# Ordering the small RWKV products G and Yo by operand shape, and alternating partition halves in M, TK and gy

## The chip, the core and the metric

One core of a Trainium2 chip runs the whole program. The metric is device time in microseconds (us) from one launch; the kernel before was timed three times, and one more execution was profiled. A core has a matrix engine (TensorE; PE in the rows, with its weight loads shown as PEld), a vector engine (DVE), a scalar engine (ACT), a third elementwise engine (POOL) and a queue engine (SP) that issues most DMAs. Each engine works through its own instruction list in order and waits on semaphores for the others. Products are written to PSUM, from where DVE and ACT read them.

## What is computed

One transformer layer on a sequence of 256 tokens with model width 2048: an input projection, four mixers (GLA, RG-LRU, NSA and RWKV-7), a gated merge, an output projection and a convolutional FFN. Nearly all of the arithmetic is in the big projections. The change lies in two mixers. RWKV-7 has 8 heads of width 64 and a state that is updated token by token:

```python
def step(state, inp):
    r_t, w_t, k_t, v_t, kk_t, a_t = inp
    sa = jnp.einsum('bhij,bhj->bhi', state, -kk_t)
    state = (state * w_t[:, :, None, :] + sa[..., None] * (kk_t * a_t)[:, :, None, :]
             + v_t[..., None] * k_t[:, :, None, :])
    return state, jnp.einsum('bhij,bhj->bhi', state, r_t)
```

GLA computes, chunk by chunk, `scores = einsum('bhtd,bhsd,bhtsd->bhts', qi, ki, decay)`; of it only one level of block scores (the tile gy) is touched.

## The kernel before

The projections stream weight chunks of 512 KB from HBM (`raw`). Each half chunk is split by ACT into a high part (`wh`, line 327) and by DVE into the rest (`wl`, line 328), and PE multiplies both with the activations into the tile `acc` (`group_A`). These acc products come in pairs: one of 512 columns with `wh`, one of 256 with `wl`. They fill PE for most of the program.

The RWKV recurrence is done in four chunks c = 0 to 3 of 64 tokens. The heads lie as 4 groups j times 2 partition halves par (partitions 0 to 63 and 64 to 127, the slices `H`). `rwkv_pre(c)` makes what does not depend on the state: M (per half, four products of 64 rows and 128 columns, masked by DVE into `mt`), and TK (transposes of the decayed keys, copied by ACT into `tk`). `rwkv_chain(c)` is the serial part. G is the sum of a product of `mt` with `uv` (128 rows, 64 columns) and, from c = 1 on, of `ar` (in the rows: ops) with the state `st` (64 rows, 64 columns); ACT copies it; U multiplies it with `z`; DVE and ACT copy U into `uv`; S gives the state's increment, from which DVE makes the new `st`; Yo is the output, again a sum of a product of 128 rows (`mt`) and, from c = 1 on, one of 64 rows (`st`). G and Yo each have 8 products of either kind in a chunk with state, and in chunk 0 only the 8 of 128 rows. `rwkv_pre(c + 1)` is written ahead of `rwkv_chain(c)`.

These small products are float32, and the trace shows each of them twice: 8 products are x16 in a row of the trace, once x8 in the printed instruction lists.

A scheduler sets the order on every engine: instructions carry priorities by band (loads, weight splits, evacuations, mixers, big products), and the scheduler places them by its own estimate of the time. So the mixers' products stand between the acc products, at places that can move when the source changes. Small PSUM tiles come from a pool of four banks (`self.ps`), acc tiles from another.

The lines of the profile that matter: 297 (every product through `mm`), 813 (TK), 289 (DVE tensor-tensor through `tt`, among them the new `st`), 327 and 328 (the splits), 831 (ACT's copy of G), 836 and 837 (the two copies of U into `uv`), 860 (the copy of Yo).

Of the kernel before, what the change touches and what calls it, by code (L numbers as in the profile page):

```python
# [16 lines left out]
MULT, ADD, SUB = ALU.mult, ALU.add, ALU.subtract  # L17
# [208 lines left out]
class Kern:  # L226
# [547 lines left out]
    def rwkv_pre(self, c, T):  # L774
        nc = self.nc
        ar, bk = T["ar"], T["bk"]
        cs = slice(c * 64, c * 64 + 64)
        H = (slice(0, 64), slice(64, 128))
        mt = self.sb("m4", [P, 2, 4, 128], F32, "mt")
        mask = self.cst("mM").unsqueeze(1).broadcast_to([P, 4, 128])  # L780
        for par in range(2):
            h = H[par]
            ps = self.ps("M")
            for j in range(4):
                self.mm(ps[:, j * 128:(j + 1) * 128], bk[h, j, par:par + 2, :].rearrange("p a b -> p (a b)"),
                        ar[h, j, :, :].rearrange("p a b -> p (a b)"))
            self.tt(mt[:, par], ps.rearrange("p (j t) -> p j t", j=4), mask, MULT)
        T["mt"] = mt
        T["z"], T["mt"] = self.rw_z[:, 4 * c:4 * c + 4, :], mt

        uv = self.sb("m2", [P, 4, 2, 64], F32, "uv")
        nc.gpsimd.memset(uv[0:64, :, 0, :], 0.0)
        nc.gpsimd.memset(uv[64:128, :, 1, :], 0.0)
        idn = self.cst("ident")
        for par in range(2):
            for f in range(2):
                for t in range(2):
                    o = 64 * (1 - par) + 32 * t
                    nc.vector.transpose(uv[o:o + 32, :, par, 32 * f:32 * f + 32],
                                        self.rw_v[64 * par + 32 * f:64 * par + 32 * f + 32, :, c * 64 + 32 * t:c * 64 + 32 * t + 32])  # L800
        T["uv"] = uv
        if c < 3:
            ec = self.rw_ec[:, :, c:c + 1]
            ht = self.sb("m4", [P, 4, 3, 64], F32, "ht")
            self.tt(ht[:, :, 0:2, :].rearrange("p j a s -> p j (a s)"), bk[:, :, 0:2, :].rearrange("p j a s -> p j (a s)"),
                    ec.broadcast_to([P, 4, 128]), MULT)
            nc.scalar.copy(ht[64:128, :, 2, :], ht[64:128, :, 0, :])
            tk = self.sb("m2", [P, 2, 4, 64], F32, "tk")
            for par in range(2):
                h = H[par]  # L810
                ps = self.ps("TK")[:, 0:256].rearrange("p (j d) -> p j d", j=4)
                for j in range(4):
                    nc.tensor.transpose(ps[:, j, :], ht[h, j, par:par + 2, :].rearrange("p a b -> p (a b)"), idn[h, h])
                nc.scalar.copy(tk[:, par], ps)
            T["tk"] = tk
        return T

    def rwkv_chain(self, c, T, st):
        nc = self.nc
        H = (slice(0, 64), slice(64, 128))  # L820
        ar, mt, z, uv = T["ar"], T["mt"], T["z"], T["uv"]
        g4 = lambda n: self.ps(n)[:, 0:256].rearrange("p (j s) -> p j s", j=4)
        ps = g4("G")
        for j in range(4):
            for par in range(2):
                h = H[par]
                self.mm(ps[h, j, :], mt[:, par, j, 0:64], uv[:, j, par, :], start=True, stop=(st is None))
                if st is not None:
                    self.mm(ps[h, j, :], ar[h, j, 0, :], st[h, j, :], start=False, stop=True)
        g = self.m1("G")  # L830
        nc.scalar.copy(g, ps)
        ps = g4("U")
        for j in range(4):
            for h in H:
                self.mm(ps[h, j, :], z[h, j, :], g[h, j, :])
        nc.vector.tensor_copy(uv[0:64, :, 0, :], ps[0:64])
        nc.scalar.copy(uv[64:128, :, 1, :], ps[64:128])
        new = None
        if c < 3:
            tk = T["tk"]  # L840
            ps = g4("S")
            for j in range(4):
                for par in range(2):
                    self.mm(ps[H[par], j, :], tk[:, par, j, :], uv[:, j, par, :])
            new = self.sb("st", [P, 4, 64], F32, "st")
            if st is None:
                nc.vector.tensor_copy(new, ps)
            else:
                sd = self.m1("sd")
                ec = self.rw_ec[:, :, c:c + 1]  # L850
                self.tt(sd, st, ec.broadcast_to([P, 4, 64]), MULT)
                self.tt(new, sd, ps, ADD)
        ps = g4("Yo")
        for j in range(4):
            for par in range(2):
                h = H[par]
                self.mm(ps[h, j, :], uv[:, j, par, :], mt[:, par, j, 64:128], start=True, stop=(st is None))
                if st is not None:
                    self.mm(ps[h, j, :], st[h, j, :], ar[h, j, 1, :], start=False, stop=True)
        nc.scalar.copy(self.rw_y[:, :, c * 64:c * 64 + 64], ps)  # L860
        return new

# [174 lines left out]
    def gla(self):  # L1037
        nc = self.nc
        H = (slice(0, 64), slice(64, 128))
        qk, b = self.gl_qk, self.gl_b  # L1040
        t = self.m4("glt")
# [3 lines left out]
        st = [self.m1("gst", 4) for _ in range(2)]  # L1045
        idb = self.cst("eye64").unsqueeze(1).broadcast_to([P, 4, 64])

        def scores(Q, K):
            out = [self.ps("gs")[:, 0:256].rearrange("p (a t) -> p a t", a=4) for _ in range(2)]
            for j in range(2):  # L1050
                for tl in range(2):
                    for odd in range(2):
                        for par in range(2):
                            o = odd ^ par
                            sl = slice(tl * 128 + 64 * o, tl * 128 + 64 * o + 64)
                            self.mm(out[par][H[o], 2 * j + tl, :], K[H[par], j, sl], Q[H[par], j, sl])
            return out

        ps = scores(qk[:, 0:2, :], qk[:, 2:4, :])
        for par in range(2):  # L1060
            self.tt(st[par], ps[par], idb, MULT)
        blk, st = st, [self.m2("gst", 4) for _ in range(2)]
# [3 lines left out]
        for lv in range(8):  # L1066
            m = 1 << lv
            bv = b.rearrange("p j (n m) -> p (j n) m", m=2 * m)
            e = self.m2("ge")
            ev = e.rearrange("p j (n m) -> p (j n) m", m=2 * m)  # L1070
            self.tt(ev, bv, bv[:, :, m - 1:m].broadcast_to([P, 256 // m, 2 * m]), SUB)
            self.act(e, e, AF.Abs)
            self.act(e, e, AF.Exp, scale=-1.0 / 16)
            qe = self.m4("qe")
            self.tt(qe[:, 0:2, :], qk[:, 0:2, :], e, MULT)
            self.tt(qe[:, 2:4, :], qk[:, 2:4, :], e, MULT)
            if lv == 6:
                for par in range(2):
                    h = H[par]
                    ps = self.ps("gy")[0:64, 0:256].rearrange("p (a t) -> p a t", a=4)  # L1080
                    for j in range(2):
                        for tl in range(2):
                            s0 = tl * 128
                            self.mm(ps[:, 2 * j + tl, :], qe[h, 2 + j, s0:s0 + 64], qe[h, j, s0 + 64:s0 + 128])
                    nc.vector.tensor_copy(st[par][0:64, :, 64:128], ps)
            elif lv < 6:
                ps = scores(qe[:, 0:2, :], qe[:, 2:4, :])
                mask = self.gm[:, lv:lv + 1, :].broadcast_to([P, 4, 64])
                for par in range(2):
                    nc.vector.copy_predicated(blk[par], mask, ps[par])  # L1090
                    if lv == 5:
                        for o, h in enumerate(H):
                            nc.scalar.copy(st[par][h, :, 64 * o:64 * o + 64], blk[par][h])
            else:
                for par in range(2):
                    h = H[par]
                    ps = self.ps("gx")[:, 0:256].rearrange("p (j t) -> p j t", j=2)
                    for j in range(2):
                        self.mm(ps[:, j, :], qe[h, 2 + j, 0:128], qe[h, j, 128:256])
                    nc.scalar.copy(sx[:, 2 * par:2 * par + 2, :], ps)  # L1100
        o = self.m4("go")
        v = self.gl_v
        for j in range(2):
            ps = self.ps("go")
# [449 lines left out]
```

## Time and profile before

| | |
|---|---|
| time, three runs | 1580.47, 1581.78, 1582.03 us (median 1581.78) |
| the profiled execution | 1582.63 us, of which 1580.8 us from first to last instruction |
| PE busy | 1562.0 us (99%) |
| DVE, ACT busy | 1238.8 us (78%), 962.7 us (61%) |
| mean granted TensorE clock | 0.991 |

The profile is of one execution. A matmul's row shows its start and how long it was under way; matmuls overlap, so a stretch in which PE is called busy may hold many products or few. What a group of products costs is read from its first start to the start of the next group. PEclk is the granted clock as a share of full speed (1.00 is 2.4 GHz, 0.50 is 1.2 GHz).

### The profile page before, as it was taken

What the parts mean: (1) busy time and instruction counts of PE and PEld (TensorE: products, weight loads), DVE (VectorE), ACT (ScalarE), POOL (GpSimd) and SP (SyncE); (2) the same over time, 40 slices, a digit from 0 to 9 for tenths busy, and PEclk for the clock granted to TensorE, in tenths of its full rate; (3) what the DMA queues carried; (4) which work ended last, traced back from release to release, by engine and by line L of the source; (5) the groups of instructions that cost most, each with busy time, mean ns of one, the idle gap of its engine ahead of it and who ended that gap; (6) DMA issues with size and microseconds to landing.
All of it is one profiled execution on the core that took longest, in us unless ns stands there. A gap on an engine that the chain in (4) does not pass through costs nothing.

```text
span 1580.8 us, 27481 instructions
## 1 busy us (share of the span) xinstructions
PE 1562.0 (99%) x10062; PEld 1413.0 (89%) x10062; DVE 1238.8 (78%) x2132; ACT 962.7 (61%) x1705; POOL 38.7 (2%) x60
## 2 busy tenths in 40 slices
PE   8999999999899999999999999999999999999998
PEld 7999888888799899899999999999999999999998
DVE  8799986476977677777787888886688886788875
ACT  6787654256665476656665666664466664566653
POOL 3000000000000000000001100000000000000000
PEclk9999999999999999999999999999999999999999
DMA  7756663245456755466676666666666666666664
GB/s 265 242 171 199 203 193 114 75 157 176 154 171 201 275 186 180 148 201 200 201 248 202 204 202 198 208 199 201 200 201 201 201 201 201 202 201 202 200 224 129
DMA packets 95800, 305.79 MB, mean 193 GB/s; under 512 B 20021, under 2 KB 20789, under 8 KB 95664
## 3 DMA queue, kind: packets, MB, share of 16 engines
q1 hardware_dynamic: 94448, 299.60, 59.9%
q0 software_dynamic: 1216, 4.43, 0.8%
q8 instruction: 79, 1.29, 0.3%
q14 instruction: 57, 0.47, 0.1%
HBM read 300.32 MB, written 3.67 MB: 192 GB/s over the span
## 4 chain that ended last, share of the span: by engine, by line
PE 95%; DVE 2%; ACT 1%; issue 1%; DMA 1%; SPq 0%; DVEq 0%; ACTq 0%
PE acc L297 89%; PE G L297 1%; PE Yo L297 1%; DVE wl L328 1%; DVE qe L289 0%; PE M L297 0%; PE no L297 0%; DMA raw<-in_wf_r 0%; PE r L297 0%; PE c L297 0%; ACT wh L327 0%; DVE th L289 0%; PE sc L297 0%; ACT ge L283 0%; PE ptp L1332 0%
## 5 line engine op out<-in xcount | busy, mean ns | idle before, releaser
L297 PE MATMUL acc<-h,wh 128*128 128x512 f32 x3008 | 1001.9, 385 | 3.0 <-DVE th L289 3.0
L327 ACT CAST wh<-raw 128x512 fp32r<-128x512 f32 x1096 | 673.6, 620 | 516.1 <-PE acc L297 490.8
L328 DVE TENSOR_TENSOR wl<-raw,wh 128x512 fp32r<-128x512 f32 x1096 | 757.7, 698 | 278.7 <-ACT wh L327 272.1
L297 PE MATMUL acc<-h,wl 128*128 128x256 f32 x3008 | 826.7, 275 | 0.0
L297 PEld LDWEIGHTS acc<-h,wh 128*128 128x128 f32 x3008 | 571.7, 190 | 85.3 <-DVE th L289 3.5
L297 PEld LDWEIGHTS acc<-h,wl 128*128 128x128 f32 x3008 | 580.5, 193 | 3.8 <-issue 1.6
L297 PE MATMUL acc<-f,wh 128*128 128x512 f32 x704 | 230.7, 382 | 0.0
L297 PE MATMUL acc<-f,wl 128*128 128x256 f32 x704 | 191.9, 273 | 0.0
L297 PEld LDWEIGHTS acc<-f,wh 128*128 128x128 f32 x704 | 133.1, 189 | 18.5
L297 PEld LDWEIGHTS acc<-f,wl 128*128 128x128 f32 x704 | 135.2, 192 | 0.0
L297 PE MATMUL acc<-mg,wh 128*128 128x512 f32 x256 | 83.9, 382 | 0.0
L286 DVE SCALAR_TENSOR_TENSOR u<-u,prm,u 128x254 f32<-128x254 f32 (+1 forms) x176 | 80.8, 480 | 0.5
L297 PE MATMUL acc<-mg,wl 128*128 128x256 f32 x256 | 69.5, 273 | 0.0
L297 PEld LDWEIGHTS acc<-mg,wh 128*128 128x128 f32 x256 | 48.2, 189 | 6.7
L289 DVE TENSOR_TENSOR xres<-xres,acc 128x512 f32<-128x512 f32 (+1 forms) x66 | 44.0, 668 | 10.0 <-PE acc L297 7.9
L283 ACT ACTIVATE u<-u,prm 128x256 f32<-128x256 f32 x88 | 48.1, 594 | 2.7 <-DVE u L289 0.8
L297 PEld LDWEIGHTS acc<-mg,wl 128*128 128x128 f32 x256 | 49.1, 192 | 0.1
L297 PE MATMUL acc<-wh,h 128*128 128x512 f32 (+1 forms) x128 | 32.2, 340 | 0.0
L289 DVE TENSOR_TENSOR u<-u,rs 128x512 f32<-128x512 f32 x44 | 30.1, 684 | 0.0
L289 DVE TENSOR_TENSOR u<-u,acc 128x512 f32<-128x512 f32 x44 | 29.9, 680 | 0.0
L380 ACT COPY u<-acc 128x512 f32<-128x512 f32 x44 | 25.5, 579 | 0.0
L297 PEld LDWEIGHTS acc<-wh,h 128*128 128x128 f32 x128 | 23.2, 202 | 2.1 <-issue 0.4
(399 smaller groups left out, 1240.9 us busy)
## 6 DMA issues: line engine op xcount, KB each, us to landing
raw<-in_w_up SPq DMA_DIRECT2D x176, 512.0 KB, 4.2
raw<-in_w_gate SPq DMA_DIRECT2D x128, 512.0 KB, 4.0
raw<-in_w_down SPq DMA_DIRECT2D x88, 512.0 KB, 4.3
raw<-in_w_branch SPq DMA_DIRECT2D x32, 512.0 KB, 3.8
raw<-in_w_out SPq DMA_DIRECT2D x32, 512.0 KB, 4.4
raw<-in_wf_k SPq DMA_DIRECT2D x8, 512.0 KB, 4.6
raw<-in_wf_misc SPq DMA_DIRECT2D x8, 512.0 KB, 4.0
raw<-in_wf_lx SPq DMA_DIRECT2D x8, 512.0 KB, 4.2
```

The source lines that it names most:

```text
L283: return self.nc.scalar.activation(out, in_, func, bias=bias, scale=scale, **kw)
L286: return self.nc.vector.scalar_tensor_tensor(out, in0, scalar, in1, op0=op0, op1=op1)
L289: return (eng or self.nc.vector).tensor_tensor(out, a, b, op=op)
L297: return self.nc.tensor.matmul(out, lhsT, rhs, start=start, stop=stop, **kw)
L327: nc.scalar.copy(wh, rb)
L328: nc.vector.tensor_tensor(wl, rb, wh.bitcast(F32), op=SUB)
L380: self.nc.scalar.copy(dst, ps[0:rows, :, 0])
```

## The change

In G and Yo the products of 128 rows are all written first and those of 64 rows after them, where they alternated before. All 8 products of the first kind and then all of the second add into one PSUM bank; so that a later product does not clear what others have summed, only the first product in either partition half (j = 0) has the start flag, and the rest add to or overwrite what stands there. In M, TK and gy the two tiles of the two partition halves are taken from the pool together, and the products alternate between the halves (j outside, par inside), with the copies behind all products.

```diff
         mask = self.cst("mM").unsqueeze(1).broadcast_to([P, 4, 128])
+        pm = [self.ps("M") for _ in range(2)]
+        for j in range(4):
+            for par in range(2):
+                h = H[par]
+                self.mm(pm[par][:, j * 128:(j + 1) * 128], bk[h, j, par:par + 2, :].rearrange("p a b -> p (a b)"),
+                        ar[h, j, :, :].rearrange("p a b -> p (a b)"))
         for par in range(2):
-            h = H[par]
-            ps = self.ps("M")
-            for j in range(4):
-                self.mm(ps[:, j * 128:(j + 1) * 128], bk[h, j, par:par + 2, :].rearrange("p a b -> p (a b)"),
-                        ar[h, j, :, :].rearrange("p a b -> p (a b)"))
-            self.tt(mt[:, par], ps.rearrange("p (j t) -> p j t", j=4), mask, MULT)
+            self.tt(mt[:, par], pm[par].rearrange("p (j t) -> p j t", j=4), mask, MULT)
...
+            pt = [self.ps("TK")[:, 0:256].rearrange("p (j d) -> p j d", j=4) for _ in range(2)]
+            for j in range(4):
+                for par in range(2):
+                    h = H[par]
+                    nc.tensor.transpose(pt[par][:, j, :], ht[h, j, par:par + 2, :].rearrange("p a b -> p (a b)"), idn[h, h])
             for par in range(2):
-                h = H[par]
-                ps = self.ps("TK")[:, 0:256].rearrange("p (j d) -> p j d", j=4)
-                for j in range(4):
-                    nc.tensor.transpose(ps[:, j, :], ht[h, j, par:par + 2, :].rearrange("p a b -> p (a b)"), idn[h, h])
-                nc.scalar.copy(tk[:, par], ps)
+                nc.scalar.copy(tk[:, par], pt[par])
...
+        heads = [(j, par, H[par]) for j in range(4) for par in range(2)]
         ps = g4("G")
-        for j in range(4):
-            for par in range(2):
-                h = H[par]
-                self.mm(ps[h, j, :], mt[:, par, j, 0:64], uv[:, j, par, :], start=True, stop=(st is None))
-                if st is not None:
-                    self.mm(ps[h, j, :], ar[h, j, 0, :], st[h, j, :], start=False, stop=True)
+        for j, par, h in heads:
+            self.mm(ps[h, j, :], mt[:, par, j, 0:64], uv[:, j, par, :], start=(j == 0), stop=(st is None), skip_group_check=True)
+        if st is not None:
+            for j, par, h in heads:
+                self.mm(ps[h, j, :], ar[h, j, 0, :], st[h, j, :], start=False, stop=True, skip_group_check=True)
...
         ps = g4("Yo")
-        for j in range(4):
-            for par in range(2):
-                h = H[par]
-                self.mm(ps[h, j, :], uv[:, j, par, :], mt[:, par, j, 64:128], start=True, stop=(st is None))
-                if st is not None:
-                    self.mm(ps[h, j, :], st[h, j, :], ar[h, j, 1, :], start=False, stop=True)
+        for j, par, h in heads:
+            self.mm(ps[h, j, :], uv[:, j, par, :], mt[:, par, j, 64:128], start=(j == 0), stop=(st is None), skip_group_check=True)
+        if st is not None:
+            for j, par, h in heads:
+                self.mm(ps[h, j, :], st[h, j, :], ar[h, j, 1, :], start=False, stop=True, skip_group_check=True)
```

gy is changed as M is: two tiles, par innermost, and the two DVE copies behind the eight products.

The lists of SP and POOL are the same in both kernels. Those of PE, DVE and ACT differ only in the RWKV stretch (and in the eight gy products); behind it they are the same, row by row.

The first place is PE's list at G of chunk 1, ahead of which stand the TK products of chunk 2. Before:

```order
L813 MATMUL TK_3244<-cstt,ht_3240 128x64 x4
L813 MATMUL TK_3250<-cstt,ht_3240 128x64 x4
L297 MATMUL G_3256<-uv_3146,mt_3133 64x64
L297 MATMUL G_3256<-st_3204,ops_1045 64x64
L297 MATMUL G_3256<-uv_3146,mt_3133 64x64
L297 MATMUL G_3256<-st_3204,ops_1045 64x64
L297 MATMUL G_3256<-uv_3146,mt_3133 64x64
L297 MATMUL G_3256<-st_3204,ops_1045 64x64
```

The list goes on in this way to 16 G products in all. The same place of the changed kernel:

```order
L814 MATMUL TK_3244<-cstt,ht_3240 128x64 x2
L814 MATMUL TK_3245<-cstt,ht_3240 128x64 x2
L814 MATMUL TK_3244<-cstt,ht_3240 128x64
L814 MATMUL TK_3245<-cstt,ht_3240 128x64
L814 MATMUL TK_3244<-cstt,ht_3240 128x64
L814 MATMUL TK_3245<-cstt,ht_3240 128x64
L297 MATMUL G_3256<-uv_3146,mt_3133 64x64 x8
L297 MATMUL G_3256<-st_3204,ops_1045 64x64 x8
L297 MATMUL acc_2953<-h_292,wl_3035 128x256
```

The sixteen G products have become two runs of eight.

The second place is PE's list from S of chunk 1 to G of chunk 2 (M_3318 and M_3324 or M_3319 are the two halves of M of chunk 3). Before, seven rows from the start of it:

```order
L297 MATMUL S_3286<-uv_3146,tk_3160 64x64
L297 MATMUL Yo_3299<-mt_3133,uv_3146 64x64
L297 MATMUL Yo_3299<-ops_1045,st_3204 64x64
L297 MATMUL M_3318<-ops_1059 128x128 x2
L297 MATMUL S_3286<-uv_3146,tk_3160 64x64 x7
L297 MATMUL Yo_3299<-mt_3133,uv_3146 64x64
L297 MATMUL Yo_3299<-ops_1045,st_3204 64x64
```

Six more alternations of Yo follow, then the other two products of M_3318, the four of M_3324, six acc products, and G_3341 in alternation. The same place of the changed kernel:

```order
L297 MATMUL S_3286<-uv_3146,tk_3160 64x64
L297 MATMUL Yo_3299<-mt_3133,uv_3146 64x64
L297 MATMUL M_3318<-ops_1059 128x128 x3
L297 MATMUL S_3286<-uv_3146,tk_3160 64x64 x7
L297 MATMUL Yo_3299<-mt_3133,uv_3146 64x64 x7
L297 MATMUL Yo_3299<-ops_1045,st_3204 64x64 x8
L297 MATMUL M_3319<-ops_1059 128x128 x3
L297 MATMUL M_3318<-ops_1059 128x128
L297 MATMUL M_3319<-ops_1059 128x128
L297 MATMUL G_3341<-uv_3229,mt_3216 64x64 x8
L297 MATMUL G_3341<-st_3295,ops_1052 64x64 x8
```

Yo has become two runs too, M does not alternate throughout but has runs of three, and G_3341 follows M at once. At S and Yo of chunk 2 G of chunk 3 follows Yo in the same way.

The third place is DVE's list around its copy of U of chunk 1 into `uv` (uv_3146<-U_3275), on which S waits on PE; one piece of the difference, - before and + after:

```order
+L328 TENSOR_TENSOR wl_3551<-raw_3536,wh_3550 128x512
 L289 TENSOR_TENSOR sd_3296<-st_3204,ec_1036 128x256
-L328 TENSOR_TENSOR wl_3551<-raw_3536,wh_3550 128x512
 L328 TENSOR_TENSOR wl_3565<-raw_3562,wh_3564 128x512
-L836 COPY uv_3146<-U_3275 64x4x64
 L328 TENSOR_TENSOR wl_3577<-raw_3562,wh_3576 128x512
 L289 TENSOR_TENSOR th_2812<-th_2812,acc_2953 128x512
 L328 TENSOR_TENSOR wl_3591<-raw_3588,wh_3590 128x512
 L289 TENSOR_TENSOR th_2812<-th_2812,rs_442 128x512
+L839 COPY uv_3146<-U_3275 64x4x64
```

The copy stands four rows later, and PE has 28 acc products between U and S of this chunk, where it had 19.

## Rows read from the trace of the kernel before

**Rows 1.** The page's head and its busy times by engine.

```profile
span 1580.8 us, 27481 instructions
PE 1562.0 (99%) x10062; PEld 1413.0 (89%) x10062; DVE 1238.8 (78%) x2132; ACT 962.7 (61%) x1705; POOL 38.7 (2%) x60
```

**Rows 2.** The page's chain that ended last, by engine.

```profile
PE 95%; DVE 2%; ACT 1%; issue 1%; DMA 1%; SPq 0%; DVEq 0%; ACTq 0%
```

**Rows 3.** Windows: stretch, length, busy us (instructions) by engine, clock, DMA share, GB/s.

```profile
230.00:330.00 100.00, 99.72 (x791) 83.08 (x791) 57.16 (x110) 37.47 (x73) 2.08 (x6) 0.93 0.33 106
395.00:440.00 45.00, 39.55 (x398) 34.28 (x398) 39.98 (x72) 27.79 (x53) 1.08 (x2) 0.92 0.50 156
600.00:1580.00 980.00, 976.40 (x5952) 895.15 (x5950) 772.58 (x1269) 593.32 (x1026) 14.65 (x15) 1.00 0.63 199
```

**Rows 4.** PE timeline, G of chunk 1: start us, us, then the product.

```profile
266.02 0.33 PE L297 MATMUL G<-uv,mt 128*64 128x64 f32 x2
266.28 0.33 PE L297 MATMUL G<-st,ops 64*64 64x64 f32 x2
...
269.88 0.32 PE L297 MATMUL G<-st,ops 64*64 64x64 f32 x2
270.13 0.79 PE L297 MATMUL acc<-h,wh 128*128 128x512 f32 x1
```

**Rows 5.** PE timeline, G of chunk 0 and the product behind it.

```profile
249.25 0.69 PE L297 MATMUL G<-uv,mt 128*64 128x64 f32 x16
249.86 0.48 PE L297 MATMUL acc<-h,wh 128*128 128x512 f32 x1
```

**Rows 6.** PE timeline, U of chunk 0 and the product behind it.

```profile
253.55 0.68 PE L297 MATMUL U<-G,Z 64*64 64x64 f32 x16
254.16 0.38 PE L297 MATMUL acc<-yb,wl 128*128 128x256 f32 x1
```

**Rows 7.** PE timeline, chunk 1: S, the last seven alternations of Yo, M.

```profile
280.60 0.68 PE L297 MATMUL S<-uv,tk 128*64 128x64 f32 x14
281.12 0.28 PE L297 MATMUL Yo<-mt,uv 128*64 128x64 f32 x2
...
284.66 1.17 PE L297 MATMUL M<-ops 64*128 64x128 f32 x12
285.76 0.48 PE L297 MATMUL acc<-h,wh 128*128 128x512 f32 x1
```

**Rows 8.** PE timeline, M of chunk 1, half after half.

```profile
243.30 1.71 PE L297 MATMUL M<-ops 64*128 64x128 f32 x16
244.94 0.38 PE L297 MATMUL acc<-h,wl 128*128 128x256 f32 x1
```

**Rows 9.** Windows around the stretches of halved clock, columns as in rows 3.

```profile
266.70:270.10 3.40, 3.40 (x28) 2.49 (x27) 0.64 (x2) 0.13 (x1) 0.00 (x0) 1.00 0.79 271
270.10:273.50 3.40, 3.40 (x13) 2.91 (x12) 0.00 (x0) 0.94 (x2) 0.00 (x0) 0.50 0.02 8
290.60:294.00 3.40, 3.40 (x13) 2.80 (x13) 0.69 (x1) 0.99 (x2) 0.00 (x0) 0.50 0.00 0
311.10:314.50 3.40, 3.40 (x12) 2.92 (x13) 0.80 (x2) 1.48 (x3) 0.00 (x0) 0.50 0.00 0
239.40:242.80 3.40, 3.40 (x12) 2.95 (x12) 3.24 (x10) 0.84 (x2) 0.00 (x0) 0.50 0.00 0
427.10:433.90 6.80, 6.04 (x19) 5.22 (x20) 6.34 (x13) 4.70 (x9) 0.54 (x1) 0.50 0.55 174
```

**Rows 10.** DVE timeline, the new state behind S of chunk 1.

```profile
281.38 0.41 DVE L289 TENSOR_TENSOR st<-sd,S 128x256 f32<-128x256 f32 x1
```

**Rows 11.** Timeline, chunk 2: the copies of U and S behind them.

```profile
297.10 0.42 DVE L836 COPY uv<-U 64x256 f32<-64x256 f32 x1
297.61 0.37 ACT L837 COPY uv<-U 64x256 f32<-64x256 f32 x1 [1.19 <-DVE uv L836]
300.72 0.34 PE L297 MATMUL S<-uv,tk 128*64 128x64 f32 x4
```

More of the change, by code (lines that the diff above doesn't have):

```diff
@@ L1077, in gla @@
             if lv == 6:
-                for par in range(2):
[L1079 to L1085, printed above, removed]
+                py = [self.ps("gy")[0:64, 0:256].rearrange("p (a t) -> p a t", a=4) for _ in range(2)]
+                for j in range(2):
+                    for tl in range(2):
+                        s0 = tl * 128
+                        for par in range(2):
+                            h = H[par]
+                            self.mm(py[par][:, 2 * j + tl, :], qe[h, 2 + j, s0:s0 + 64], qe[h, j, s0 + 64:s0 + 128])
+                for par in range(2):
+                    nc.vector.tensor_copy(st[par][0:64, :, 64:128], py[par])
             elif lv < 6:
```

## The prediction

> **What bounds the kernel now.** I read the page from the top. PE is busy for 1562.0 of 1580.8 us, DVE for 78% and ACT for 61% [rows 1], and the chain that ended last runs over PE for 95% of the span [rows 2]. So time taken off PE's list comes off the end, if no other engine is late in that place. The windows by stretch say where that holds: from 230 to 330 us, where the RWKV chain runs, PE is busy for 99.72 of 100 us, DVE for 57.16, ACT for 37.47 and DMA for a third, and the granted clock is 0.93, below 1.00 [rows 3]. Behind 600 us PE has 3.6 us of idle time in 980 [rows 3]. Only in GLA's stretch (395 to 440 us) does PE idle for 5.45 of 45 us with DVE as busy as PE [rows 3]; of the change only gy's eight products lie there.
>
> "Busy" hides what the change is about, so I went on to the timeline. In G of chunk 1, products of 128 rows and of 64 rows alternate: the first starts at 266.02, the next kind at 266.28, and the acc product behind the sixteen at 270.13 [rows 4]. That is 4.11 us, 0.257 for each change of shape. G of chunk 0 has eight products of 128 rows without a change: from 249.25 to the acc product at 249.86, 0.61 us [rows 5]. U has eight of 64 rows, with the partition half changing from product to product into one bank, as the second half of the new G has: 253.55 to 254.16, 0.61 us [rows 6]. So PE overlaps small products of one shape and empties itself between two shapes.
>
> The second thing to see is the clock [rows 9]. From 266.7 to 270.1, all alternation, PE got through 28 small products at a granted 1.00; from 270.1 to 273.5 the clock is 0.50, 1.2 GHz. The same stands behind G of chunk 2 (290.6) and of chunk 3 (311.1). Each of these halved stretches is 3.4 us long and does the work of 1.7.
>
> **The change, part by part.** *G, chunks 1 to 3.* Before 4.11 us [rows 4]. After, by the order, eight of one shape and eight of the other: 0.61 [rows 5] + 0.61 [rows 6] = 1.22. Gain 2.89 each, 8.7 in all. *Yo, chunks 1 to 3.* Seven alternations take from 281.12 to 284.66, 3.54 us, or 0.506 each [rows 7]; eight are 4.05. After, the first kind stands directly behind S, which has the same shape: fourteen S rows take from 280.60 to 281.12, 0.037 each [rows 7], so sixteen rows of Yo take about 0.5 to 0.6, and the second kind 0.61 [rows 6]: 1.15. Gain 2.9, and 0.3 less in chunk 3, where an acc product cuts the first run: 8.4 in all.
>
> *M.* Half after half, 16 rows take from 243.30 to 244.94, 1.64 us [rows 8]. Where before had two products of one half and four of the other left over, 12 rows with the halves beside each other took from 284.66 to 285.76, 1.10 us [rows 7]. After, M of chunks 0 and 1 alternate and should take 1.1: gain 0.5 each. M of chunks 2 and 3 do not: the order shows three products of one half, then S and Yo, then three of the other, so I take the lone three at two fifths to three fifths of 1.64 and the rest at 1.1: a loss of 0.4 each. Together +0.2, between -1 and +1. *TK and gy.* The eight transposes of chunk 0 stood in two pieces between acc products and are now in one: two changes of shape less, 0.5 by [rows 4]. TK of the other chunks was contiguous already, and gy has 16 rows of one shape, 0.61 by [rows 6] in whatever order; at nothing, since nothing stands between them. The removed start flags belong to instructions that stay: nothing.
>
> *The clock.* The three halved stretches follow on PE passing mostly through changes of shape [rows 9]; with these gone PE is dense there, as it is in S, M and U, and I expect all three to go: 3 x 1.7 = 5.1. From below: 0, if they come back elsewhere. From above: the stretches at 239.4 and 427.1 [rows 9] may also fall otherwise, since all behind moves; they cost 1.7 and 3.4 now.
>
> *Waits that the order could add.* With PE faster, the covers shrink, in three places. First, G of chunks 2 and 3 now follows Yo and M without acc products, and needs the new state. S ends into Yo at 281.12 [rows 7] and DVE made the state from 281.38 to 281.79 [rows 10], 0.67 us later. Ahead of the state-dependent half PE has in the new order the rest of Yo (about 1.1) and the first half of G (0.5), in chunk 2 M as well: 1.6 or more. Hidden; with one or two more DVE instructions in front (0.52 us on average [rows 3]) nearly bare, and then at most 1 us in each of two chunks. Second, M and TK take two of the four small PSUM banks at once: S, Yo and the two of M hold all four when G of chunk 2 asks for one. S's bank is freed by that same DVE instruction, so it is the same 0.67 us against Yo and M. Third, the copy of U of chunk 1 stands four DVE rows later (some 2 us by that average, if all ran behind U), and ACT's half of it follows. In chunk 2 ACT was done at 297.98 and S began at 300.72 [rows 11], 2.7 us to spare; in chunk 1 PE has nine acc products more in between, some 1.2 us (13 in 3.4 us at half the clock [rows 9]). Hidden on balance, and if not, 1 to 2 us, once or twice. Behind PE's wait nothing but PE's own list queues up; the weight splits go on. I add 0 for all three, and keep a loss of 4 us for the range.
>
> *The sum.* 8.7 + 8.4 + 0.2 + 0.5 + 5.1 = 22.9 us. The profiled execution took 1582.63, so 1559.7; the median of the runs, 1581.78, lies 0.85 lower, and against it I get 1558.9: I say 1559.
>
> **A rule that speaks against it.** The second run of G and of Yo changes the partition half with each product, and all of them write to one PSUM bank. U does exactly that, and its 16 rows took 0.61 us [rows 6], 0.035 to 0.04 each. The Trainium skill, TensorEngine Tiling (Array Packing), section "Gotcha 1: PSUM Pressure", says that different row tiles cannot access the same PSUM bank at the same time. If products of the two halves had to take turns in this way, that page would leave the second run no overlap; U's row disagrees, and I go by it. The rule as a mechanism of this kernel is a rival below.
>
> **The rivals.** *The clock stays.* Halved stretches remain or turn up elsewhere, because PE sees ever more small products and fewer acc products between them. For: one halved stretch lies at 239.4, behind no alternation [rows 9]. Against: the other three of the chain stand right behind G. With 1.7 to 5.1 of gain lost: 1561 to 1564.
>
> *More clock than I count.* The stretch at 239.4 goes as well, since TK no longer cuts it up, and GLA's 6.8 us [rows 9] fall otherwise: 1554 to 1557.
>
> *No overlap in the second run.* If the products of the two halves took turns, a run would cost at most what M costs half after half, 1.64 us for its 16 rows [rows 8], in place of 0.61; six runs lose 6.2: 1565. U's row is against it.
>
> *The change moves PE's work and not the end.* If the splits or DMA set the pace in the stretch, PE would wait for what it gained: 1577 to 1582. Against: DVE's 57 us, ACT's 37 and DMA's 33 fit into 77 us as well [rows 3].
>
> *Slower.* The clock falls in the dense small products themselves: in the new order S, Yo, M and G of chunks 1 and 2 stand together for some 4 us without an acc product. If that halved the clock, and it kept falling, the loss would have to exceed the 17.8 us of the other terms and the 6.8 that the four stretches cost now: 24.6 us, or 49 us of halved clock between 230 us and the chain's end, half of it. From that point on the kernel is slower; with 55 us it would be about 1585. Against: dense S, Yo and M of chunk 1 ended at 285.76 [rows 7], and the next halved stretch, at 290.6, follows G's alternation [rows 9].
>
> **How the numbers follow.** My forecast (1556.5 to 1561) has 0.62; the clock stays 0.15; more clock 0.14; no overlap 0.03; work moved and not the end 0.04; slower 0.02. The predicted time is 1559. From 1554 to 1564 the range holds the first three but for their edges, some 0.85 of the chance, and within it the wait terms of 4 us; it leaves the last three out. About 0.2%, 3 us, is what a measurement of this kernel can tell from no change: faster by more than that 0.94, within it 0.04, slower 0.02.
>
> **What would show it.** In the profile after: G of chunks 1 to 3 taking about 1.2 us each from first start to the next group, Yo about 1.15, M of chunks 0 and 1 about 1.1; a granted clock above 0.97 in the stretch of the chain, without halved stretches behind G; the chain's end (ACT's copy of Yo of chunk 3) some 22 us earlier, and everything behind it by the same amount. Wrong I would be if PE shows idle time in front of S or of G's second half, if G's second run takes 1.7 us, or if the clock in the stretch is 0.93 or less; also if PE's idle time behind 330 us grew by what was won ahead of it.

## The result, and the profile after

The changed kernel took 1553.72 us (median of four runs, 1551.89 to 1554.72), the kernel before in the same set 1581.12 (four runs, 1577.91 to 1582.03). The ratio is 0.9822, with a 95% interval of 0.9804 to 0.9841: 1.8% faster. The prediction was 1559, with a range down to 1554, and the measured time lies 0.3 us below it: the direction and the mechanism came out, the gain is some 5 us larger than worked out.

One execution was profiled again. It took 1554.55 us, where the profiled execution of before took 1582.63: 28.1 us less. The page's head and its chain, which answer to [rows 1] and [rows 2]:

```profile
span 1552.8 us, 27480 instructions
PE 1534.4 (99%) x10062; PEld 1392.5 (90%) x10062; DVE 1238.2 (80%) x2132; ACT 961.6 (62%) x1705; POOL 38.5 (2%) x60
...
PE 95%; DVE 3%; ACT 1%; issue 1%; DMA 0%; SPq 0%; DVEq 0%; ACTq 0%
```

The counts by engine are the same as before. PE was called busy 27.6 us longer before, for the same 10062 rows; DVE and ACT have not changed. The kernel is bound by PE's list as it was.

Windows show where the time went. The first three of the changed kernel answer to [rows 3]: the first is 20 us shorter and holds more rows of products (823 for 791), the other two begin 20 us earlier, and GLA's clock is 0.92 as before. The fourth runs from the first product of P (which opens the RWKV work) to the end of Yo of chunk 3, the whole of what the change touches but gy:

```profile
230.00:310.00 80.00, 80.00 (x823) 70.59 (x822) 60.67 (x113) 40.42 (x78) 2.08 (x6) 1.00 0.44 138
375.00:420.00 45.00, 40.58 (x385) 35.66 (x386) 35.29 (x65) 27.09 (x50) 1.08 (x2) 0.92 0.45 147
580.00:1552.00 972.00, 968.41 (x5902) 887.69 (x5900) 767.52 (x1259) 588.32 (x1020) 14.65 (x15) 1.00 0.62 199
225.80:300.20 74.40, 74.40 (x845) 65.42 (x844) 57.18 (x110) 35.93 (x70) 2.08 (x6) 1.00 0.45 142
```

The same stretch of before, from P's first product to Yo's end:

```profile
227.20:326.30 99.10, 98.81 (x842) 82.34 (x842) 57.61 (x111) 35.84 (x69) 1.79 (x6) 0.93 0.34 109
```

The same work (845 and 842 rows; a few records are missing in a trace) takes 74.40 us for 99.10, at a granted clock of 1.00 for 0.93. So 24.8 of the 28.1 us lie here (24.7 by the rounded windows). DVE and ACT do the same 57 and 36 us of work in the shorter stretch, and PE is busy throughout: the views of PE's waits list none from 220 to 345 us. Of the rest, P begins 1.3 us earlier (at 225.82 for 227.16), ahead of anything that the change touches, and 1.8 us come behind Yo, 1.7 of them because a halved stretch of before at 567.1 has no counterpart. GLA's halved stretch is still there.

The products themselves, in the timeline of PE. G of chunk 1 and the product ahead of it, which answers to [rows 4]:

```profile
262.97 0.47 PE L814 MATMUL TK<-cstt,ht 64*128 64x64 f32 x8
263.36 0.69 PE L297 MATMUL G<-uv,mt 128*64 128x64 f32 x16
263.98 0.68 PE L297 MATMUL G<-st,ops 64*64 64x64 f32 x16
264.59 0.38 PE L297 MATMUL acc<-h,wl 128*128 128x256 f32 x1
```

From 263.36 to 264.59 are 1.23 us, where alternation took 4.11. The second run, whose products change the partition half each time and write to one bank, takes 0.61 (263.98 to 264.59), like U in [rows 6]. The Trainium skill says in "Gotcha 1: PSUM Pressure" (TensorEngine Tiling (Array Packing)) that different row tiles cannot access the same PSUM bank at the same time. Here the halves write to their own partitions of one bank, and the second run takes no longer than the first, 0.61 us: if products take turns, it costs nothing beyond that.

S, Yo, M and G behind them, in chunk 1 and the start of chunk 2, which answers to [rows 7]:

```profile
273.79 0.33 PE L297 MATMUL S<-uv,tk 128*64 128x64 f32 x2
273.95 0.28 PE L297 MATMUL Yo<-mt,uv 128*64 128x64 f32 x2
274.16 0.93 PE L297 MATMUL M<-ops 64*128 64x128 f32 x6
275.02 0.62 PE L297 MATMUL S<-uv,tk 128*64 128x64 f32 x13
275.43 0.27 PE L297 MATMUL Yo<-mt,uv 128*64 128x64 f32 x1
275.48 0.22 PE L297 MATMUL S<-uv,tk 128*64 128x64 f32 x1
275.53 0.64 PE L297 MATMUL Yo<-mt,uv 128*64 128x64 f32 x13
276.10 0.68 PE L297 MATMUL Yo<-ops,st 64*64 64x64 f32 x16
276.71 1.16 PE L297 MATMUL M<-ops 64*128 64x128 f32 x10
277.79 0.69 PE L297 MATMUL G<-uv,mt 128*64 128x64 f32 x16
278.41 0.68 PE L297 MATMUL G<-st,ops 64*64 64x64 f32 x16
```

Yo from 275.53 to 276.71 is 1.18 us (its first row, at 275.43, overlaps the end of S, which has the same shape). The six rows of M that stand alone (three products of one half) take 0.86 us, 0.143 a row; the ten behind Yo 1.08. M of chunk 0, which alternates throughout:

```profile
231.66 1.16 PE L297 MATMUL M<-ops 64*128 64x128 f32 x16
232.75 0.48 PE L297 MATMUL acc<-h,wh 128*128 128x512 f32 x1
```

It takes 1.09 us, as does M of chunk 1, where half after half took 1.64 [rows 8].

The new state, which G's second run needs, in DVE's timeline; it answers to [rows 10], and the bracket is DVE's idle time and what ended it:

```profile
275.74 0.42 DVE L289 TENSOR_TENSOR st<-sd,S 128x256 f32<-128x256 f32 x1 [1.18 <-PE S L297]
```

The state is ready at 276.16, and G's second run starts at 278.41, 2.2 us later: hidden, as was counted.

Added up over the stretch (each group from its first start to the next group's start, time at half the clock counted half): G 12.81 to 4.29 us, Yo 12.60 to 4.93, M 6.65 to 6.08, TK 1.57 to 1.09 and a wait of 0.28 in front of it gone, the rest (ZP, S, acc) 0.5 less: some 18.0 us of PE's list. The other 6.8 of the 24.8 are four halved stretches of 3.4 us each, three behind G and one at 239.4 [rows 9], all gone.

### The profile page after: what moved, and what is told of

It reads as the page before. It is cut to its first block, busy times and chain, and to the rows that moved or that the text cites. A ratio compares the mean times of both kernels' runs of the same rounds, so it can differ in the third digit from the quotient of the medians.

```text
span 1552.8 us, 27480 instructions
## 1 busy us (share of the span) xinstructions
PE 1534.4 (99%) x10062; PEld 1392.5 (90%) x10062; DVE 1238.2 (80%) x2132; ACT 961.6 (62%) x1705; POOL 38.5 (2%) x60
## 4 chain that ended last, share of the span: by engine, by line
PE 95%; DVE 3%; ACT 1%; issue 1%; DMA 0%; SPq 0%; DVEq 0%; ACTq 0%
PE acc L297 90%; DVE wl L328 1%; DVE qe L289 0%; PE no L297 0%; PE M L297 0%; PE c L297 0%; PE r L297 0%; PE Yo L297 0%; DVE h L286 0%; DMA raw<-in_wf_r 0%; PE sc L297 0%; PE G L297 0%; ACT ge L283 0%; PE ptp L1335 0%; DVE th L289 0%
## 5 line engine op out<-in xcount | busy, mean ns | idle before, releaser
L283 ACT ACTIVATE th<-th 128x512 f32<-128x512 f32 (+1 forms) x33 | 21.3, 644 | 4.3 <-DVE th L289 4.2
```

Source lines behind the costliest of these rows:

```text
L283: return self.nc.scalar.activation(out, in_, func, bias=bias, scale=scale, **kw)
```

## The experiments

Three theories were to be told apart. **By number**: the products that change shape cost their list time, and they also bring the halved clock, in proportion to how many there are, whether G's or Yo's. **G alone**: the clock falls because of G, behind which the halved stretches stood. **Elsewhere**: the extra gain comes from the start flags, from the new places of M and TK, or from the variation between executions.

Since the halved stretches lie in other places from run to run, one profile doesn't settle a matter of the clock. For every run the mean granted clock is known, so I take (1 - clock) x span as the time lost to the clock, and the mean of the times less that loss as the list. (The clock of a run is given to 0.001, which is 1.6 us of its span.) This takes a little too much off where changes of shape run at half the clock (below). Each set has its own runs of the kernel before:

| kernel | median us (runs) | before, median (runs) | ratio and interval | mean clock | lost | time less loss |
|---|---|---|---|---|---|---|
| before, first set | 1581.12 (23) | | | 0.9914 | 13.5 | 1568.1 |
| flags_only | 1583.45 (10) | 1581.12 (23) | 1.0008 [0.9996, 1.0021] | 0.9901 | 15.7 | 1567.5 |
| mtkgy_only | 1579.43 (12) | 1581.12 (23) | 0.9985 [0.9971, 1.0000] | 0.9914 | 13.5 | 1565.7 |
| gyo_only | 1556.30 (4) | 1581.12 (23) | 0.9839 [0.9821, 0.9856] | 0.9980 | 3.1 | 1553.3 |
| after_again | 1553.79 (5) | 1581.12 (23) | 0.9820 [0.9803, 0.9837] | 0.9982 | 2.8 | 1550.8 |
| before, second set | 1582.83 (11) | | | 0.9911 | 14.1 | 1568.0 |
| g_only | 1563.54 (6) | 1582.83 (11) | 0.9894 [0.9874, 0.9914] | 0.9958 | 6.5 | 1558.4 |
| yo_only | 1564.59 (6) | 1582.83 (11) | 0.9894 [0.9872, 0.9917] | 0.9967 | 5.2 | 1559.8 |
| pairs | 1559.29 (4) | 1582.83 (11) | 0.9859 [0.9842, 0.9876] | 0.9982 | 2.7 | 1556.5 |
| g_twice | 1602.85 (4) | 1582.83 (11) | 1.0132 [1.0114, 1.0149] | 0.9842 | 25.2 | 1577.3 |
| before, third set | 1582.28 (9) | | | 0.9910 | 14.2 | 1566.9 |
| late_half_first | 1551.44 (5) | 1582.28 (9) | 0.9812 [0.9790, 0.9833] | 0.9980 | 3.1 | 1547.7 |
| after_third | 1555.23 (4) | 1582.28 (9) | 0.9838 [0.9818, 0.9858] | 0.9975 | 3.9 | 1551.1 |

**flags_only**: the kernel before, with the start flags of the change and nothing else (the same in Yo).

```diff
-self.mm(ps[h, j, :], mt[:, par, j, 0:64], uv[:, j, par, :], start=True, stop=(st is None))
+self.mm(ps[h, j, :], mt[:, par, j, 0:64], uv[:, j, par, :], start=(j == 0), stop=(st is None), skip_group_check=True)
```

> G and Yo alternate between the shapes as before, and only the start flags are those of the change (one clearing product per half); the order of every engine is that of the kernel before. If the changes of shape cost the time: G of chunk 1 takes 4.1 us again, and the time is that of before within 3 us. If the clearing products cost it: G falls towards 1.2 us and the time by 17 us or more.

The lists of all engines are in the order of before, and the time is that of before (1.0008, the interval takes in 1). The flags are worth nothing. Its G of chunk 1 shows single changes of shape at either clock, from the timeline of PE (the line "..." stands for the changes between):

```profile
262.99 0.33 PE L297 MATMUL G<-uv,mt 128*64 128x64 f32 x2
263.25 0.33 PE L297 MATMUL G<-st,ops 64*64 64x64 f32 x2
263.50 0.33 PE L297 MATMUL G<-uv,mt 128*64 128x64 f32 x2
...
266.07 0.47 PE L297 MATMUL G<-uv,mt 128*64 128x64 f32 x2
266.47 0.47 PE L297 MATMUL G<-st,ops 64*64 64x64 f32 x2
```

The first step leads from a product to the one that adds onto the same place in PSUM, the second to a product with a place of its own, and at full clock they take 0.26 and 0.25 us. So what costs is the change of shape, and not that a sum waits for its first part. At 266.07 a step is 0.40, where the windows give a clock of 0.51; so part of a step does not follow the clock. That window, and the longest halved stretch of this execution:

```profile
266.00:272.90 6.90, 6.90 (x26) 5.64 (x25) 0.69 (x1) 0.99 (x2) 0.00 (x0) 0.51 0.09 30
283.10:296.70 13.60, 13.60 (x60) 10.52 (x60) 2.78 (x5) 1.36 (x3) 0.00 (x0) 0.50 0.00 0
```

The second is 13.6 us in one piece, four times any that the profile of before shows in the chain, for a kernel with the same lists: how the loss falls differs by execution, and three stretches of one profile were a small sample of it.

**mtkgy_only** and **gyo_only**: the two halves of the change, each by itself: the former has G and Yo as before, the latter M, TK and gy as before.

> M, TK and gy as changed, G and Yo as before. If the shape changes in G and Yo carry the gain: 0.5 to 3 us faster than before (M and TK 0.7, and 1.7 more if the halved stretch at 239 us goes), the halved stretches behind G still there. If the alternating halves carry a good part of it (through the clock or through M): 5 to 10 us faster.

> G and Yo as changed, M, TK and gy as before. If the shape changes carry the gain: 21 to 27 us faster, G 1.2 us and Yo 1.1 us each, no halved stretch behind G; the one at 239 us stays if it comes from TK standing in pieces, and is gone if it only depends on where things fall. If the alternating halves carry a good part: 16 to 20 us faster.

> The changed kernel once more beside the others. 26 to 29 us faster than before on the same chip. If the number of halved stretches outside the chain's stretch depends on where things fall and not on the program, the halved stretches in GLA differ from those of the first profile, and the clock of the timed runs varies by some thousandths, with about 1.7 us for each halved stretch.

G and Yo carry nearly all: gyo_only is 24.8 us below before by the medians, and its clock is that of the changed kernel. M, TK and gy alone leave the clock at 0.9914 and save 1.7 us by the medians, with an interval that reaches to no gain (1.0000), and 2.4 by time less loss; added to G and Yo they save 2.5 either way (1556.30 to 1553.79, 1553.3 to 1550.8). That is more than the 0.7 that I had for them, and by the unchanged clock it is list time. The profile of gyo_only has one halved stretch, in GLA, and none near 239.4, where before had one: with TK still in pieces it is gone, so the pieces alone do not bring it. "Elsewhere" falls for the clock: with M, TK and gy in their new places and G and Yo as before, nothing of the loss is gone. Windows over the RWKV stretch and what follows, of flags_only, mtkgy_only and after_again in this order:

```profile
225.00:345.00 120.00, 118.92 (x937) 99.13 (x938) 71.23 (x133) 47.85 (x90) 2.08 (x6) 0.90 0.35 110
225.00:345.00 120.00, 120.00 (x948) 100.56 (x947) 71.92 (x134) 48.92 (x92) 2.08 (x6) 0.90 0.35 113
225.00:345.00 120.00, 119.28 (x1096) 105.07 (x1096) 93.82 (x171) 64.41 (x119) 2.08 (x6) 1.00 0.49 157
```

At 0.90 over 120 us, 12 us are lost in this stretch in either kernel with both alternations, where the profile of before shows four halved stretches, 6.8 us lost [rows 9]. In the kernels with G and Yo in runs (gyo_only, pairs and late_half_first too) the clock in it is 1.00.

**g_only** and **yo_only**: the changed kernel with Yo (in yo_only: G) written in alternation as before.

> The changed kernel with Yo alternating as before; G, M, TK and gy as changed. Without the clock: G is worth 8.5 us and M and TK about 1.5, so 10 us faster than before. If every alternation of shapes draws the clock alike, half of the clock's loss goes as well (the mean granted clock rises from 0.991 to about 0.995): 15 us faster, with halved stretches left behind Yo. If only G's alternation draws it, as the first profile of before had it: clock 0.998, 20 us faster, no halved stretch in the chain. If the clock has nothing to do with the alternations: 10 us faster at a clock of 0.991.

> The changed kernel with G alternating as before; Yo, M, TK and gy as changed. Without the clock 9.5 us faster than before. If every alternation draws the clock alike: 14 to 15 us faster, clock about 0.995, halved stretches behind G. If only G's does: 10 us faster at a clock of 0.991. If the clock has nothing to do with it: 10 us faster too, but with halved stretches elsewhere than behind G.

Either way about half of the list gain and over half of the clock gain comes: 6.5 and 5.2 us lost, between 14.1 and some 3. By the medians the kernels are 19.3 and 18.2 us faster, more than the 15 and the 14 to 15 expected for alternations that all draw the clock alike. So G is not special, and "G alone" falls. In the profile of g_only, the slowest of its six runs, where G is dense, the halved stretches stand behind Yo's alternations, which run from 275.2 to 278.7, 293.1 to 297.3 and 309.4 to 313.6. Its windows:

```profile
279.30:286.20 6.90, 6.90 (x52) 5.98 (x50) 2.31 (x4) 1.19 (x3) 0.00 (x0) 0.51 0.00 0
296.40:303.20 6.80, 6.80 (x50) 5.81 (x49) 0.69 (x1) 1.36 (x3) 0.00 (x0) 0.50 0.03 10
313.50:316.90 3.40, 3.40 (x12) 2.91 (x11) 1.57 (x3) 2.04 (x4) 0.30 (x1) 0.50 0.00 0
```

In the profile of yo_only, the fastest of its six runs, one halved stretch is left in the chain, from the end of an alternation of G (261.5 to 265.9) on:

```profile
265.20:268.60 3.40, 3.40 (x13) 2.80 (x14) 0.37 (x1) 0.99 (x2) 0.00 (x0) 0.51 0.12 49
```

The times of single runs fall into two groups in both kernels, 1560.4 to 1563.7 us at a clock of 0.997 to 1.000 (seven runs) and 1568.1 to 1570.6 at 0.992 to 0.996 (five): the alternations make a halved stretch likely, and don't fix it.

**pairs**: the changed kernel with G and Yo in four runs of two products of either kind, one in either partition half. There are eight runs, where before had sixteen and the change two.

```diff
-for j, par, h in heads:
-    self.mm(ps[h, j, :], mt[:, par, j, 0:64], uv[:, j, par, :], start=(j == 0), stop=(st is None), skip_group_check=True)
-if st is not None:
-    for j, par, h in heads:
-        self.mm(ps[h, j, :], ar[h, j, 0, :], st[h, j, :], start=False, stop=True, skip_group_check=True)
+for j0 in range(4):
+    for j, par, h in heads[2 * j0:2 * j0 + 2]:
+        self.mm(ps[h, j, :], mt[:, par, j, 0:64], uv[:, j, par, :], start=(j == 0), stop=(st is None), skip_group_check=True)
+    if st is not None:
+        for j, par, h in heads[2 * j0:2 * j0 + 2]:
+            self.mm(ps[h, j, :], ar[h, j, 0, :], st[h, j, :], start=False, stop=True, skip_group_check=True)
```

> The changed kernel with the shapes of G and Yo changing after every two products (8 runs in place of 2, where before had 16). If the price is one per change of shape (2.9 us for the 14 changes saved, 0.206 each), G of chunk 1 takes 1.22 + 6 x 0.206 = 2.5 us and the kernel loses 7.4 us against the change before the clock. If what costs is that a product finds none of its own shape beside it to overlap with, runs of two give nearly all back: G 1.3 to 1.8 us, a loss of 1 to 3 us. Clock: 0.998 if the halved stretches need the bare alternation, 0.994 or less if fewer products per us is enough.

G of chunk 1 in its timeline of PE, the first three runs, the last and the product behind it:

```profile
264.82 0.34 PE L297 MATMUL G<-uv,mt 128*64 128x64 f32 x4
265.08 0.33 PE L297 MATMUL G<-st,ops 64*64 64x64 f32 x4
265.35 0.34 PE L297 MATMUL G<-uv,mt 128*64 128x64 f32 x4
...
266.66 0.33 PE L297 MATMUL G<-st,ops 64*64 64x64 f32 x4
266.93 0.38 PE L297 MATMUL acc<-h,wl 128*128 128x256 f32 x1
```

2.11 us for eight runs, 0.264 each. A run of two products costs what a run of one costs (0.257 [rows 4]), and a run of eight 0.61. So in these short runs the partner in the other half comes free; whether a second product in the same half would, was not run. The 2.11 us lie between the two figures expected, 2.5 for a fixed price of each change and 1.3 to 1.8 if it were only the missing neighbour. That brings two thirds of the list's gain (time less loss is 11.5 us below before, where the change is 17.3 below it), and all of the clock's: 2.7 us lost, and no halved stretch in the chain of its profile. The Trainium skill says under "Key Properties" (TensorEngine Tiling (Array Packing)) that a change of tiling mode drains TensorE; 0.257 for a run of one and 0.264 for a run of two agree with a price for the change itself.

The number of changes alone does not settle the loss to the clock: in G and Yo of chunks 1 to 3 pairs has 48 runs, g_only and yo_only have 54. Its four runs are few for this, as seven of the twelve of those two were fast as well.

**g_twice**: the kernel before with G of chunks 1 to 3 done twice, in alternation (the second pass clears the first, so G is unchanged).

```diff
+for _ in range(1 if st is None else 2):
     for j in range(4):
         for par in range(2):
```

> The kernel before with the products of G of chunks 1 to 3 done twice in alternation, the second time anew, so the result stays; the alternations of G are twice as long. By the PE's list alone 3 x 4.11 = 12.3 us slower than before. If the clock's loss comes from the alternations in proportion (10.4 us for 25 us of them): 17 to 18 us slower and a clock of 0.988 or less. If the halved stretches have nothing to do with them: 12 us slower at 0.991. If PE had time to spare in that stretch: less than 10 us slower.

20.0 us slower by the medians, where a loss in proportion would have made it 17 to 18. The loss to the clock rises from 14.1 to 25.2, and time less loss by 9.3, where three more passes of 4.11 us would be 12.3; the difference is about what the loss takes too much, since these steps ran partly at half the clock. In its windows each halved stretch has tripled against [rows 9] (270.1, 290.6, 311.1), and stands in and behind the second pass:

```profile
266.70:276.90 10.20, 10.20 (x46) 7.75 (x45) 0.00 (x0) 0.91 (x2) 0.00 (x0) 0.50 0.01 4
294.00:304.20 10.20, 10.20 (x46) 7.73 (x46) 0.69 (x1) 0.99 (x2) 0.00 (x0) 0.50 0.01 2
321.30:331.50 10.20, 10.20 (x45) 7.86 (x45) 1.29 (x2) 1.48 (x3) 0.00 (x0) 0.50 0.00 0
```

With this the loss is in order of the bare alternations, product by product, in G and Yo: none (after, gyo_only, pairs) some 3 us, one of the two 5 to 6.5, both 13.5 to 15.7, one and a half times both 25. It grows faster than in proportion; of "By number" it holds that G and Yo both count, but not the proportion, and what in the alternation draws the clock is not shown.

**late_half_first** and **after_third**: the changed kernel with the halves in the other order in G, Yo and S, and the changed kernel beside it. The scheduler then puts S, Yo and M in single runs, where the change has a lone product of S and of Yo and three of M ahead of the rest.

```diff
-heads = [(j, par, H[par]) for j in range(4) for par in range(2)]
+heads = [(j, par, H[par]) for j in range(4) for par in (1, 0)]
...
-                for par in range(2):
+                for par in (1, 0):
```

> The changed kernel with the second partition half first within each pair in G, S and Yo. The first product of S then waits for the later of the two copies of U, and the scheduler's order keeps S, Yo and M of the next chunk each in one piece (in the changed kernel M's three products of one half split S and Yo in chunks 0 and 1). If the price per shape change and per lone half holds: S, Yo and M of chunk 1 go from 4.00 to 2.7 us, those of chunk 0 from 3.40 to 2.1, in all 2 to 3 us faster than the changed kernel, 1551 us. If S now waits on PE for the second copy: nothing gained, and idle time in front of S.

> The changed kernel beside the one above on the same chip: 26 to 29 us faster than before, the clock of its runs between 0.996 and 1.000, no halved stretch in the chain's stretch; at most one or two of the halved stretches behind it, at places that differ from run to run.

Chunk 1 and the start of chunk 2 in its timeline of PE:

```profile
272.88 0.69 PE L297 MATMUL S<-uv,tk 128*64 128x64 f32 x16
273.39 0.64 PE L297 MATMUL Yo<-mt,uv 128*64 128x64 f32 x16
273.96 0.68 PE L297 MATMUL Yo<-ops,st 64*64 64x64 f32 x16
274.57 1.16 PE L297 MATMUL M<-ops 64*128 64x128 f32 x16
275.66 0.69 PE L297 MATMUL G<-uv,mt 128*64 128x64 f32 x16
276.28 0.68 PE L297 MATMUL G<-st,ops 64*64 64x64 f32 x16
```

M is 1.09 us in one run, where it took 0.86 + 1.08. Over the chain M goes from 6.08 to 4.56 us, Yo from 4.93 to 4.15 and S from 1.81 to 1.54, 2.6 in all. The kernel took 1551.44 us (1547.88 to 1551.97), the changed kernel on the same chip 1555.23 (1553.15 to 1556.27): 3.8 us less, without overlap, where 2 to 3 were expected. Some 0.8 of it is clock by the table. It is the fastest version found, 0.9812 [0.9790, 0.9833] of before.

## Why the prediction was off by 5 us

**What bounds the kernel** held: time taken off PE's list came off the end, all of it. The chain's stretch is 24.8 us shorter, its end (ACT's copy of Yo of chunk 3) lies 26.1 us earlier (300.31 for 326.45), and of this nothing was given back behind it. The rival that the change moves work and not the end is out, since PE has no wait in the stretch.

**G and Yo** held: 8.5 us for 8.7 and 7.7 for 8.4. Yo gained less since a lone product of Yo (chunk 1 above) still pays for a run of its own. **M** gained 0.6 for 0.2 (before, the four rows that stood alone took 0.63, from 279.97 to 280.60, more than the quarter of 1.64 that the forecast loss implies, so less was lost there), **TK** 0.5 for 0.5 and a wait besides. M, TK and gy together are worth about 2.4 in the runs with only them, for 0.7; of that the profiles show 0.6 + 0.5 + 0.28, and some 1 us is not placed; mtkgy_only's twelve runs range over 11 us, so it may be scatter. The whole list is 18.0 us between the two profiles and 17.3 by time less loss (1568.1 to 1550.8), for 17.8. **The waits** that the order could add did not come: 0 for 0. **No overlap in the second run** is out, at 0.61 us.

**The step that failed is the clock**: "I expect all three to go: 3 x 1.7 = 5.1." The mechanism held, all three went; the term was mis-sized. The runs put it at 10.7 us (13.5 lost before, 2.8 after), twice the forecast. I took one profile for the kernel's usual loss, and only what stood directly behind G. But the profile of before shows 0.991, 14 us lost, of which these three stretches are 5.1: the row with the mean clock in the table of before was enough to ask where the other 9 were. Most of it stands in halved stretches at 31 us (1.7 lost), 239.4 (1.7), 427.1 (3.4) and 567.1 (1.7). And in the chain that profile was a mild one, 6.8 us lost where flags_only and mtkgy_only, with the same alternations, lost 12. Alternations of Yo draw the clock too, as g_only shows, and the stretches fall in other places from one execution to the next. The rival "more clock than I count" is nearest to what happened, though in the profile after only its stretch at 239.4 is gone and GLA's 6.8 us stand; its lower end of 1554 lies 0.3 us above the measured median. 17.3 of list and 10.7 of clock make 28.0, for 27.4 by the medians.

**Slower** by the clock in dense small products is out: where S, Yo, M and G stand together for 5 us (273.79 to 279.02 after), the clock stays at 1.00.

What stays open is whether the halved stretches outside the chain hang on the change, and what in the alternations draws the clock. GLA's 6.8 us stand in the profile after, half of that in after_third's, nothing in those of pairs and after_again; one near 540 or 567 us stands in some, one at 31 us in six of the twelve.

## What to carry to other kernels

Where two kinds of small products alternate on TensorE, write them in runs by shape, with the partition halves alternating inside a run: a change cost about 0.26 us here for a run of one or of two, and sixteen passes in one run 0.61. A row that says PE is busy does not show this; the distance between starts does. Take the price of a halved clock from the mean granted clock of all runs, not from the stretches that one profile happens to show, and look at the order that the scheduler makes, since a single product that slips ahead of its run pays for a run of its own.

## What the runs showed of the hardware

A run of one fp32 product of 64 columns took 0.257 us between changes of shape, one of two products in different partition halves 0.264, and one of eight 0.61. At half the clock a change took 0.40 us for 0.26, not twice as much.

The clock fell to 0.50 behind alternations in which PE was "busy" throughout, and not behind dense runs of the same products: 13.5 to 15.7 us lost with alternation in both G and Yo, 25.2 with G's doubled, some 3 with none. Four executions with runs of two, at the same price for each run but half as many, lost no more than those with none.
